# A hybrid encoder block on one core: modulation tiles added a step after their request, decay broadcasts pinned, solve copies reordered

## The chip, the cores and the metric

The kernel runs on one core of one Trainium2 chip. The metric is the device time of one execution in microseconds. A run of the kernel gives one time; several runs are compared by their median. One further execution was profiled, and its instructions, waits and transfers are what the views below show.

## The reference

One layer of a bidirectional encoder block for 256 tokens of width 2048, all in fp32:

```python
mod = silu(c) @ ada_w + ada_b          # 6 x 2048: shift, scale, gate for mixer and FFN
h = rms_norm(x, norm_mix_w) * (1 + scale_m) + shift_m
proj = h @ w_in                        # mLSTM q,k,v,o,i,f | delta rule q,k,v,z,beta,a | merge gates
y_a = mlstm_bidirectional(...) @ w_branch_a
y_b = gated_delta_bidirectional(...) @ w_branch_b
x = x + gate_m * ((g_a * y_a + g_b * y_b) @ w_out)
hf = rms_norm(x, norm_ffn_w) * (1 + scale_f) + shift_f
x = x + gate_f * ((silu(gt) * up) @ w_down)      # gt, up = split(hf @ w_gate_up)
return rms_norm(x, norm_final_w)
```

The delta rule has 16 heads of width 128. Per head and direction it needs a decay mask (products of the tokens' decays), the inverse of a unit triangular matrix per chunk, and products with the values.

## The kernel before, in words

**Weights.** Every weight arrives in chunks of 1 MB through three buffers with the tag `raw` (pool `st`), requested on the SP queue by `nc.sync.dma_start` (L156 in `fjob`, L183 in `tjob`). A chunk is turned into a high part by ScalarE (`wh`, L160 and L186) and a low part by VectorE (`wl`, L162 and L188), each in two halves, and TensorE takes three products per weight block (L165 to L167, L207 to L209). The SP queue issues its transfers in the order in which they are written, and a transfer into a buffer waits until the last reader of what lay there is done.

**Modulation.** The parts of `mod` that are needed later (2 to 5, sixteen tiles of 1 MB each) are made in the background. `ada_parts` requests a tile (L117) into one of the same three `raw` buffers and adds it: VectorE multiplies it with the row of silu(c) and sums along the row (L121). `pump`, called after each finished chunk, calls `sums` on every `every[0]`-th call, and this advances `ada_parts` by a tile. `room[0]` says which pool, how many buffers and how many tiles may be requested ahead: the `raw` buffers with depth 1 in the delta rule and the mLSTM part and again in the feed-forward part; a pool of its own (`sr`, three buffers, depth 3) between, while `y_a` and the output projection run. With depth 1, a tile's request and its addition are written one right after the other.

**The order of the work.** What is not pinned is placed by a planner, which puts the instructions of each engine in the order in which it expects them to be ready. `order(...)` (L71) pins an instruction behind everything already written for its engine. Small closures that must not be pinned too early are kept in the list `behind` (the SiLU after a convolution `end`, the copies of a triangle's corners `corners`, the norm of an output `scaled`), and `settle` (L130) writes out what the list holds; `fjob` and `tjob` call it between the two conversions of a half.

**The delta rule** (L868 to L917) treats four groups of four heads. `gdn_conv` (L287) prepares a projected head; for the first of its three projections it allots the decay buffer `al` (two of them) and calls `decay_load` (L282), which clears its edge and broadcasts the decays from DRAM, both on GpSimd (POOL), not pinned. `gdn_phase1` (L556) makes the masks by scans on VectorE (L562 to L565), the triangles (`mi`, `mb`), stores them (`inst`, L623) and reads them back in another layout (`uu`, L626), both from POOL. `gdn_invert` (L642) solves the four heads' small triangles on VectorE. `gdn_blocks` (L673) reads the result back, and copies it into `X` and `UL` (L692, L700), pinned on ScalarE. `gdn_phase2` (L703) works on a pair of heads in nine steps; the last one calls `settle()` (L795) and transposes the result. In the loop over `n` (L901) a step of the pair is written first, then a step of the block copies, then some pieces of the next heads' projections. `every[0]` is 0 in group 0 and in the inversions and 2 in groups 1 to 3.

**After it** come the mLSTM part with `y_b` (L1057 on), `y_a`, the output projection, and the feed-forward part from L1223.

Of the kernel before, what the change touches and what calls it, by code (L numbers as in the profile page):

```python
# [52 lines left out]
def hybrid_block(ctx: ExitStack, tc: tile.TileContext, xr, nfr, crow, pk_d, cst_d, ada2, ada4, win0, winb, wint, wba, wbb, wo, wgu, wd, out, dbg=None):  # L53
# [47 lines left out]
        order(S.activation(row_c[:, g * 512 : (g + 1) * 512], pc_, AF.Silu))  # L101


    room = [(st, "raw", 3, 1)]

    def ada_parts(*parts):

        todo = [(part, b) for part in parts for b in range(KB)]  # L110
        asked = []
        while todo or asked:
            pl, tag, bufs, depth = room[0]
            while todo and len(asked) < depth:
                part, b = todo.pop(0)
                raw = pl.tile([P, D], F32, tag=tag, bufs=bufs, name=f"ada{part}_{b}")
                nc.sync.dma_start(raw, ada4[part - 2, b])  # L117
                asked.append((part, b, raw))
            part, b, raw = asked.pop(0)
            c = part * KB + b  # L120
            V.scalar_tensor_tensor(raw, raw, 1.0, row_c[:, :D], ALU.mult, ALU.mult, accum_out=mod[:, c : c + 1])  # L121
            if b == KB - 1:
                c = slice(part * KB, part * KB + KB)
                V.tensor_tensor(mod[:, c], mod[:, c], pk[:, PK_ADAB + c.start : PK_ADAB + c.stop], ALU.add)
            yield True


    behind = []

    def settle(keep=0):  # L130

        while len(behind) > keep:
            behind.pop(0)()

    background = []
    count, every = [0], [0]
# [14 lines left out]
    def fjob(name, src, done):  # L151

        ps = acc_ps.tile([P, 512], F32, tag="acc", name=f"acc_{name}")
        o = ps[:, :T]
        raw = st.tile([P, KB, P], F32, tag="raw", bufs=3, name=f"raw_{name}")
        nc.sync.dma_start(raw, src)  # L156
        for k0 in range(0, KB, 8):
            wh = st.tile([P, 8, P], F32R, tag="wh", bufs=3, name=f"wh_{name}_{k0}")
            wl = st.tile([P, 8, P], F32R, tag="wl", bufs=3, name=f"wl_{name}_{k0}")
            S.activation(wh, raw[:, k0 : k0 + 8], AF.Copy)  # L160
            settle()
            V.tensor_tensor(wl, raw[:, k0 : k0 + 8], wh.bitcast(F32), ALU.subtract)  # L162
            for k in range(8):
                kk = k0 + k
                PE.matmul(o, wh[:, k], hh[:, kk], start=kk == 0, stop=False)  # L165
                PE.matmul(o, wh[:, k], hl[:, kk], start=False, stop=False)  # L166
                PE.matmul(o, wl[:, k], hh[:, kk], start=False, stop=kk == KB - 1)  # L167
            if k0:
                pump()
                done(o)  # L170
            yield True

    def tjob(name, chunks, xh, xl, done, early=0, by_token=None, steps=1):

        raws = {}

        def halves(u, k0):  # L180
            if u not in raws:
                raws[u] = st.tile([P, 4, 512], F32, tag="raw", bufs=3, name=f"raw_{name}_{u}")
                nc.sync.dma_start(raws[u], chunks[u])  # L183
            wh = st.tile([P, 2, 512], F32R, tag="wh", bufs=3, name=f"wh_{name}_{u}_{k0}")
            wl = st.tile([P, 2, 512], F32R, tag="wl", bufs=3, name=f"wl_{name}_{u}_{k0}")
            order(S.activation(wh, raws[u][:, k0 : k0 + 2], AF.Copy), early)  # L186
            settle()
            order(V.tensor_tensor(wl, raws[u][:, k0 : k0 + 2], wh.bitcast(F32), ALU.subtract), early)  # L188
            return wh, wl

        todo = [(u, k0) for u in range(len(chunks)) for k0 in (0, 2)]
        made = []
        for i, q in enumerate(todo[:early]):
            made.append(halves(*q))
            if steps > 1 or i == early - 1:
                yield True
        ps = [acc_ps.tile([P, 512], F32, tag="acc", name=f"acc_{name}_{t}") for t in range(2)]
        last = 4 * len(chunks) - 1
        if by_token:
            todo = todo[:-2]  # L200
        for n, (u, k0) in enumerate(todo):
            wh, wl = made.pop(0) if made else halves(u, k0)
            for k in range(2):
                kk = 4 * u + k0 + k
                for t in range(2):
                    c = slice(t * P, (t + 1) * P)
                    order(PE.matmul(ps[t], xh[:, kk, c], wh[:, k], start=kk == 0, stop=False), early and steps > 1)  # L207
                    PE.matmul(ps[t], xl[:, kk, c], wh[:, k], start=False, stop=False)  # L208
                    PE.matmul(ps[t], xh[:, kk, c], wl[:, k], start=False, stop=kk == last)  # L209
            if k0:  # L210
                pump()
                if u == len(chunks) - 1:
                    done(ps)
            yield True
            if early and steps > 1:
                if n + early < len(todo):
                    made.append(halves(*todo[n + early]))
                yield True
        if by_token:
            w = [halves(len(chunks) - 1, k0) for k0 in (0, 2)]  # L220
            by_token()
            for t in range(2):
                c = slice(t * P, (t + 1) * P)
                for k in range(4):
                    kk = last - 3 + k
                    wh, wl = (a[:, k % 2] for a in w[k // 2])
                    PE.matmul(ps[t], xh[:, kk, c], wh, start=False, stop=False)
                    PE.matmul(ps[t], xl[:, kk, c], wh, start=False, stop=False)
                    PE.matmul(ps[t], xh[:, kk, c], wl, start=False, stop=kk == last)
                done(t, ps[t])  # L230
                yield True
# [49 lines left out]

    def decay_load(h):  # L282
        al = parts[h][2]
        G.memset(al[:, :, 0:8], 0.0)
        G.dma_start(al[:, :, 8:], alpha_d[:, h].partition_broadcast(P))

    def gdn_conv(h, j, ps):  # L287

# [414 lines left out]
    def gdn_phase2(g, p):  # L703
# [88 lines left out]
            po, r4 = po2[:, 2 * e * P : 2 * (e + 1) * P], hd[e][4]  # L792
            ons.append(gdn_norm(g, h, hl_, po, r4))
        yield
        settle()  # L795
        for e, on in enumerate(ons):
            h, hl_ = 4 * g + 2 * p + e, 2 * p + e
            for t in range(2):
# [84 lines left out]
    def invert(g):  # L883
        gen = gdn_invert(g)
        next(gen)
        fill(4 if g else 6)
        for _ in gen:
            fill(1)

    invert(0)  # L890
    for g in range(4):
# [7 lines left out]
        for p in range(2):  # L899
            pieces = stream(4 * g + 2 * p + 4)  # L900
            for n in range(1, 10):  # L901
                next(pairs[p], None)
                if p == 0:
                    next(blocks, None)
                for _ in range(last[n] if g == 3 else second[n] if p else after[n]):
                    next(pieces)
            for _ in pairs[p]:
# [5 lines left out]
        if g < 3:  # L913
            fills.insert(0, z_job(g + 1))
            every[0] = 0
            invert(g + 1)
    settle()  # L917
    sx.close()
# [138 lines left out]
    cores = steps(mlstm(0), mlstm(1))  # L1057
    o4s = [o_load(g) for g in range(2)]
    every[0] = 0
    fill(2)  # L1060
    next(cores)
    fill(6)
# [23 lines left out]
    mgh, mgl = big(bigC, F32R, "mgh"), big(bigC, F32R, "mgl")  # L1086
    sm_.close()
    sr_ = ExitStack()
    room[0] = (pool(sr_, "sr"), "sr", 3, 3)
    for g in range(4):  # L1090
        every[0] = (2, 1, 1, 0)[g]
# [313 lines left out]
```

## Time and profile before

| | us |
|---|---|
| runs shown: median (lowest to highest, 3 runs) | 2083.49 (2080.6 to 2085.63) |
| profiled execution | 2082.03 |
| its span, first to last instruction | 2080.3 |
| mean granted TensorE clock in it | 0.992 |

PE is TensorE, PEld its weight loads, DVE VectorE, ACT ScalarE, SP the queue engine. In the timeline and the lists a row begins with the start in us from the beginning of the span and the duration in us; what stands in brackets at its end is the time that the engine stood idle ahead of it and what ended this wait. In the list of waits, the engine and line named first waited for what stands behind the arrow; the numbers are the total in us, how many times, and the longest. `L121` is line 121 of the kernel.

### The profile page before, as it was taken

The page shows a single profiled execution, that of the slowest core. Times are in us where ns is not written, and L with a number is a line of the kernel's source. Part 1 is how long each engine was busy: PE and PEld are TensorE (multiplying, and loading weights), DVE is VectorE, ACT ScalarE, POOL GpSimd, SP SyncE. Part 2 cuts the span into 40 slices and gives each one's busy share as a digit, 9 for nine tenths or more (in the row PEclk, how much of TensorE's full clock was granted, in tenths as well). Part 3 has the DMA queues.
Part 4 walks back from the last instruction along what each step waited for, and adds up shares of the span by engine and source line. Part 5 has one row for each costly group of instructions (what it writes and reads, how often), then busy time and mean ns, then how long its engine had stood idle before and what let it go on. Part 6 is the DMA issues. An engine that isn't in the chain of part 4 may idle for free.

```text
span 2080.3 us, 27020 instructions
## 1 busy us (share of the span) xinstructions
PE 2027.5 (97%) x10374; PEld 1698.8 (82%) x10374; DVE 1398.0 (67%) x2075; ACT 1033.1 (50%) x1551; POOL 116.8 (6%) x211
## 2 busy tenths in 40 slices
PE   8999999999999999999999999999999999999998
PEld 6777789978998988889777778788888888878886
DVE  6778877877887877765676976665655654455554
ACT  3147648756764766555344334454444444444443
POOL 0002210110111001101100000200000000000000
PEclk9999999999999999999999999999999999999999
DMA  9976664557766556667885976466666665555553
GB/s 401 420 316 201 193 230 160 162 191 247 245 205 206 210 197 223 233 230 271 310 300 184 397 300 228 145 224 234 239 235 230 239 239 195 188 201 185 200 187 137
DMA packets 78963, 485.65 MB, mean 233 GB/s; under 512 B 10585, under 2 KB 15969, under 8 KB 24433
## 3 DMA queue, kind: packets, MB, share of 16 engines
q1 hardware_dynamic: 63360, 450.95, 59.7%
q0 software_dynamic: 8160, 17.88, 3.8%
q10 hardware_dynamic: 7314, 15.10, 1.9%
q8 instruction: 81, 1.33, 0.3%
q14 instruction: 48, 0.39, 0.1%
HBM read 467.07 MB, written 16.82 MB: 233 GB/s over the span
## 4 chain that ended last, share of the span: by engine, by line
PE 73%; DVE 10%; DMA 9%; ACT 4%; issue 3%; POOL 0%; SPq 0%; ACTq 0%; DVEq 0%; POOLq 0%
PE acc_up L209 4%; PE acc_up L207 4%; PE acc_up L208 4%; PE acc_d L208 4%; PE acc_d L209 4%; PE acc_d L207 4%; PE acc_gt L207 4%; PE acc_gt L208 4%; PE acc_gt L209 4%; DMA ra<-ada 3%; PE acc_o L209 2%; PE acc_o L207 2%; PE acc_o L208 2%; PE acc_b L167 2%; PE acc_b L165 2%
## 5 line engine op out<-in xcount | busy, mean ns | idle before, releaser
L188 DVE TENSOR_TENSOR wl_d<-raw_d,wh_d 128x1024 fp32r<-128x1024 f32 x88 | 107.8, 1225 | 119.9 <-ACT wh_d L186 119.9
L188 DVE TENSOR_TENSOR wl_up<-raw_up,wh_up 128x1024 fp32r<-128x1024 f32 x88 | 107.6, 1225 | 110.5 <-ACT wh_up L186 110.5
L188 DVE TENSOR_TENSOR wl_gt<-raw_gt,wh_gt 128x1024 fp32r<-128x1024 f32 x88 | 107.8, 1225 | 91.0 <-ACT wh_gt L186 91.0
L165 PE MATMUL acc_b<-hh,wh_b 128*128 128x256 f32 x576 | 165.7, 288 | 1.5 <-ACT wh_b L160 1.5
L167 PE MATMUL acc_b<-hh,wl_b 128*128 128x256 f32 x576 | 161.9, 281 | 1.4 <-DVE wl_b L162 1.4
L121 DVE SCALAR_TENSOR_TENSOR ada<-ada,crow 128x2048 f32<-128x2048 f32 x64 | 146.2, 2286 | 24.3 <-DMA ada<-ada 24.3
L186 ACT ACTIVATE wh_d<-raw_d 128x1024 fp32r<-128x1024 f32 x88 | 93.3, 1061 | 139.0 <-PE acc_d L208 134.0
L166 PE MATMUL acc_b<-hl,wh_b 128*128 128x256 f32 x576 | 160.6, 279 | 0.0
L186 ACT ACTIVATE wh_gt<-raw_gt 128x1024 fp32r<-128x1024 f32 x88 | 93.3, 1060 | 128.7 <-PE acc_gt L208 77.2
L186 ACT ACTIVATE wh_up<-raw_up 128x1024 fp32r<-128x1024 f32 x88 | 93.2, 1060 | 116.4 <-PE acc_up L208 82.9
L207 PE MATMUL acc_gt<-wh_gt,hfh 128*128 128x512 f32 x352 | 139.6, 397 | 1.0 <-ACT hfh L1218 1.0
L208 PE MATMUL acc_gt<-wh_gt,hfl 128*128 128x512 f32 x352 | 138.9, 395 | 0.0
L209 PE MATMUL acc_gt<-wl_gt,hfh 128*128 128x512 f32 x352 | 137.7, 391 | 0.0
L208 PE MATMUL acc_up<-wh_up,hfl 128*128 128x512 f32 x352 | 136.9, 389 | 0.0
L207 PE MATMUL acc_up<-wh_up,hfh 128*128 128x512 f32 x352 | 136.9, 389 | 0.0
L209 PE MATMUL acc_up<-wl_up,hfh 128*128 128x512 f32 x352 | 136.8, 389 | 0.0
L207 PE MATMUL acc_d<-wh_d,ffh 128*128 128x512 f32 x344 | 134.3, 391 | 0.0
L208 PE MATMUL acc_d<-wh_d,ffl 128*128 128x512 f32 x344 | 134.3, 390 | 0.0
L209 PE MATMUL acc_d<-wl_d,ffh 128*128 128x512 f32 x344 | 133.9, 389 | 0.0
L530 PE MATMUL first<-x,raw 128*128 128x256 f32 x512 | 114.5, 382 | 6.8 <-ACT x L524 6.4
L530 PEld LDWEIGHTS first<-x,raw 128*128 128x128 f32 x512 | 96.0, 190 | 25.2 <-ACT x L524 12.8
L165 PEld LDWEIGHTS acc_b<-hh,wh_b 128*128 128x128 f32 x576 | 109.4, 190 | 2.3 <-ACT wh_b L160 1.6
(371 smaller groups left out, 5267.1 us busy)
## 6 DMA issues: line engine op xcount, KB each, us to landing
ada<-ada SPq DMA_DIRECT2D x64, 1024.0 KB, 5.2
raw_gt<-wgu SPq DMA_DIRECT2D x44, 1024.0 KB, 4.9
raw_up<-wgu SPq DMA_DIRECT2D x44, 1024.0 KB, 4.8
raw_d<-wd SPq DMA_DIRECT2D x44, 1024.0 KB, 4.8
raw_b<-winb SPq DMA_DIRECT2D x36, 1024.0 KB, 5.0
ra<-ada SPq DMA_DIRECT2D x32, 1025.0 KB, 15.4
raw<-win SPq DMA_DIRECT2D x16, 1024.0 KB, 14.5
raw_z<-wint SPq DMA_DIRECT2D x16, 1024.0 KB, 5.0
```

The lines of the kernel that those rows point to most:

```text
L121: V.scalar_tensor_tensor(raw, raw, 1.0, row_c[:, :D], ALU.mult, ALU.mult, accum_out=mod[:, c : c + 1])
L165: PE.matmul(o, wh[:, k], hh[:, kk], start=kk == 0, stop=False)
L166: PE.matmul(o, wh[:, k], hl[:, kk], start=False, stop=False)
L167: PE.matmul(o, wl[:, k], hh[:, kk], start=False, stop=kk == KB - 1)
L186: order(S.activation(wh, raws[u][:, k0 : k0 + 2], AF.Copy), early)
L188: order(V.tensor_tensor(wl, raws[u][:, k0 : k0 + 2], wh.bitcast(F32), ALU.subtract), early)
L207: order(PE.matmul(ps[t], xh[:, kk, c], wh[:, k], start=kk == 0, stop=False), early and steps > 1)
L208: PE.matmul(ps[t], xl[:, kk, c], wh[:, k], start=False, stop=False)
L209: PE.matmul(ps[t], xh[:, kk, c], wl[:, k], start=False, stop=kk == last)
L530: PE.matmul(first[o], raw[:, o], x[:, b], start=b == 0 and o % 2 == 0, stop=b == KB - 1 and o % 2 == 1)
```

## The change

The additions move into a function of their own, with a list `asked` that outlives a step. Where the depth is now 0 (the delta rule and the mLSTM part), a step of `ada_parts` first adds the tile that was requested a step earlier and then requests the next one. Where steps are far apart, `raw_tile`, through which the weights now get their buffers, writes the addition ahead of the third buffer after the request; it is also written ahead of each further inversion, at the start of the mLSTM part and ahead of `y_a`. `decay_load` is pinned on POOL. The last step of a pair settles only the closures named `scaled`. In the loop over `n`, the step of the block copies comes ahead of the pair's.

```diff
-    room = [(st, "raw", 3, 1)]
+    room = [(st, "raw", 3, 0)]
+    asked, since = [], [0]
+
+    def add():
+        part, b, raw = asked.pop(0)
+        c = part * KB + b
+        V.scalar_tensor_tensor(raw, raw, 1.0, row_c[:, :D], ALU.mult, ALU.mult, accum_out=mod[:, c : c + 1])
+        if b == KB - 1:
+            c = slice(part * KB, part * KB + KB)
+            V.tensor_tensor(mod[:, c], mod[:, c], pk[:, PK_ADAB + c.start : PK_ADAB + c.stop], ALU.add)
 
     def ada_parts(*parts):
         todo = [(part, b) for part in parts for b in range(KB)]
-        asked = []
         while todo or asked:
             pl, tag, bufs, depth = room[0]
-            while todo and len(asked) < depth:
+            if not depth and asked:
+                add()
+            while todo and len(asked) < max(depth, 1):
                 part, b = todo.pop(0)
                 raw = pl.tile([P, D], F32, tag=tag, bufs=bufs, name=f"ada{part}_{b}")
                 nc.sync.dma_start(raw, ada4[part - 2, b])
                 asked.append((part, b, raw))
-            part, b, raw = asked.pop(0)
-            ...
+                since[0] = 0
+            if depth:
+                add()
             yield True
 
+    def raw_tile(shape, name):
+        since[0] += 1
+        if since[0] > 2 and asked and room[0][0] is st:
+            add()
+        return st.tile(shape, F32, tag="raw", bufs=3, name=name)
+
-    def settle(keep=0):
-        while len(behind) > keep:
-            behind.pop(0)()
+    def settle(keep=0, only=None):
+        now = [f for f in behind if only is None or f.__name__ == only]
+        for f in now[: len(now) - keep]:
+            behind.remove(f)
+            f()
 ...
-        G.memset(al[:, :, 0:8], 0.0)
-        G.dma_start(al[:, :, 8:], alpha_d[:, h].partition_broadcast(P))
+        order(G.memset(al[:, :, 0:8], 0.0))
+        order(G.dma_start(al[:, :, 8:], alpha_d[:, h].partition_broadcast(P)))
 ...
-        settle()
+        settle(only="scaled")
         for e, on in enumerate(ons):
 ...
             for n in range(1, 10):
-                next(pairs[p], None)
                 if p == 0:
                     next(blocks, None)
+                next(pairs[p], None)
 ...
         if g < 3:
             fills.insert(0, z_job(g + 1))
             every[0] = 0
+            if asked:
+                add()
             invert(g + 1)
```

Two more `if asked: add()` stand ahead of the mLSTM part's first `fill(2)` and ahead of the change of `room[0]` to the pool `sr`; `fjob` and `tjob` call `raw_tile` in place of `st.tile`.

More of the change, by code (lines that the diff above doesn't have):

```diff
@@ L118, in ada_parts @@
                 asked.append((part, b, raw))
-            part, b, raw = asked.pop(0)
[L120 to L124, printed above, removed]
-            yield True
-    behind = []
-    def settle(keep=0):
-        while len(behind) > keep:
-            behind.pop(0)()
+                since[0] = 0
+            if depth:
+                add()
+            yield True
+    def raw_tile(shape, name):
[3 more added lines that the diff above has]
+        return st.tile(shape, F32, tag="raw", bufs=3, name=name)
+    behind = []
+    def settle(keep=0, only=None):
[3 more added lines that the diff above has]
+            f()
     background = []
@@ L154, in fjob @@
         o = ps[:, :T]
-        raw = st.tile([P, KB, P], F32, tag="raw", bufs=3, name=f"raw_{name}")
+        raw = raw_tile([P, KB, P], f"raw_{name}")
         nc.sync.dma_start(raw, src)
@@ L181, in halves @@
             if u not in raws:
-                raws[u] = st.tile([P, 4, 512], F32, tag="raw", bufs=3, name=f"raw_{name}_{u}")
+                raws[u] = raw_tile([P, 4, 512], f"raw_{name}_{u}")
                 nc.sync.dma_start(raws[u], chunks[u])
@@ L1059, in hybrid_block @@
     every[0] = 0
+    if asked:
+        add()
     fill(2)
@@ L1088, in hybrid_block @@
     sr_ = ExitStack()
+    if asked:
+        add()
     room[0] = (pool(sr_, "sr"), "sr", 3, 3)
```

## The prediction

> **What bounds the kernel now.** I read the page first, then one table of windows by stage, then the chain of waits in the stages that the edit touches.
>
> ```profile
> PE 2027.5 (97%) x10374; PEld 1698.8 (82%) x10374; DVE 1398.0 (67%) x2075; ACT 1033.1 (50%) x1551; POOL 116.8 (6%) x211
> 480.00:600.00 120.00, 118.03 (x887) 109.50 (x886) 100.68 (x184) 84.66 (x168) 11.28 (x22) 1.00 0.69 234
> 600.00:680.00 80.00, 78.51 (x439) 67.08 (x439) 61.28 (x128) 42.11 (x65) 11.26 (x22) 1.00 0.63 202
> 680.00:800.00 120.00, 117.10 (x876) 109.82 (x875) 95.58 (x182) 84.15 (x171) 8.86 (x17) 0.97 0.60 211
> ...
> 870.00:970.00 100.00, 97.75 (x569) 85.06 (x570) 60.07 (x85) 56.23 (x109) 0.00 (x0) 0.98 0.66 234
> 970.00:1138.00 168.00, 162.66 (x714) 126.84 (x713) 110.30 (x150) 72.27 (x100) 14.70 (x24) 0.97 0.73 268
> ```
>
> The first line is the page's total; TensorE (PE) is busy 97% of the span. The window rows give a stretch and its length, then the busy time of PE, its weight loads, VectorE (DVE), ScalarE (ACT) and POOL, then the granted PE clock, the DMA share and GB/s. The modulation tiles with the new order are requested between 480 and 1138 us (none in 800 to 863). In these rows PE is idle 1.97 + 1.49 + 2.90 + 2.25 + 5.34 = 14.0 us, and the clock below 1.00 costs another 0.03 x 120 + 0.02 x 100 + 0.03 x 168 = 10.6 us. So some 25 us, 1.2% of the time, is all that the edit could ever win. What it could lose has no such ceiling. Next: where in these stages the loss sits.
>
> ```profile
> 740.00:760.00 20.00, 17.76 (x141) 17.36 (x140) 15.86 (x31) 12.91 (x27) 2.70 (x5) 0.91 0.48 175
> 760.00:780.00 20.00, 20.00 (x161) 19.87 (x161) 13.80 (x25) 13.05 (x23) 0.00 (x0) 0.92 0.61 211
> 860.00:880.00 20.00, 18.27 (x100) 15.57 (x99) 11.95 (x15) 9.11 (x16) 2.00 (x4) 0.91 0.65 230
> 980.00:1000.00 20.00, 16.74 (x71) 13.52 (x70) 11.26 (x12) 7.49 (x8) 4.85 (x9) 0.96 1.02 390
> 1000.00:1020.00 20.00, 20.00 (x90) 16.70 (x89) 13.53 (x21) 9.06 (x12) 2.53 (x4) 0.86 0.82 308
> ```
>
> The worst place in the delta rule is 740 to 780: 2.24 us idle, and a clock of 0.91 and 0.92 that costs 0.09 x 20 + 0.08 x 20 = 3.4 us. The chain of waits tells what came ahead of it:
>
> ```profile
> 729.93 2.22 DVE ada L121 x2
> 732.17 8.68 DMA raw_b<-winb
> ...
> 746.69 2.21 DVE ada L121 x2
> 748.90 1.14 DVE wl_b L162
> ```
>
> Read it downward: an addition of a modulation tile (ada, L121) ends, and only then can a weight transfer start in the buffer it leaves; the transfer takes 8.68 us, and later a second addition stands 2.21 us ahead of the conversion (wl_b, L162) that PE wants. Both additions are what the edit moves.
>
> **The change, part by part.**
>
> *The additions.* Their number stays; the last 16 of them lie in the feed-forward part, where the depth is still 1 and the order is as it was. No work is removed or added.
>
> ```profile
>   DMA ada<-ada: 24.3, 14
> SPq L156 <- DVE ada L121: 50.2, 11, 10.4
> SPq L183 <- DVE ada L121: 83.7, 30, 10.8
> 1016.67 2.29 DVE L121 SCALAR_TENSOR_TENSOR ada<-ada,crow 128x2048 f32<-128x2048 f32 x1 [4.70 <-DMA ada<-ada]
> ```
>
> One addition is 2.29 us of DVE. It made DVE stand still 24.3 us in 14 waits for its own transfer (first line, idle before the addition), the longest 4.70 us at 1016.67. The two SPq lines count the other side: 41 times a weight transfer on the SP queue was released by an addition. That queue issues in order, so everything behind such a transfer waits too. After the edit an addition is written two weight chunks later, behind both chunks' conversions, so it should no longer stand ahead of a conversion, but it also gives its buffer back later.
>
> By stage. *680 to 800:* I take the 2.24 us gap and the 3.4 us of clock as won, **-5.6 us**; bounds from -6.5 (all idle and clock of the stage, 2.90 + 3.6) to a loss that the first rival prices. *480 to 600:* an addition stands in the chain here too (515.14):
>
> ```profile
> 515.14 1.18 DVE ada L121
> 894.15 5.78 DMA ada<-ada
> 976.71 18.97 DMA bc<-mal_d
> ```
>
> Of 1.97 us idle I take a third, **-0.7** (bounds 0 and -1.97). *870 to 970:* most of the 2.25 us idle is the 1.73 in 860 to 880, where the solve's result is read back; what the ada transfer at 894.15 ends is the smaller rest, **-0.4** (0 to -0.5). *970 to 1138:* the 3.26 us idle in 980 to 1000 belongs to the broadcast of the mLSTM decay (18.97 us) and stays. The rest is 5.34 - 3.26 = 2.1 us idle and a clock loss of 0.14 x 20 = 2.8 us in 1000 to 1020, in which the 4.70 us wait lies. DVE is otherwise under-used here (110.30 of 168), so an addition may well keep its place; I take a third, **-1.6** (0 to -4.9).
>
> *Price of the later release.* Between 680 and 800 a modulation tile's buffer is wanted by the next weight transfer almost at once:
>
> ```profile
> ACT wh_b L160 <- DMA raw_b<-winb: 8.1, 5, 4.3
> 679.70 0.33 SPq L117 DMA_DIRECT2D ada<-ada  x1
> ...
> 748.93 1.47 SPq L156 DMA_DIRECT2D raw_b<-winb  x2
> ...
> 783.25 0.33 SPq L117 DMA_DIRECT2D ada<-ada  x1
> ```
>
> ACT stood still 8.1 us in 5 waits for such transfers, so there is little slack. An addition behind one more pair of conversions (wl_b, 2 x 1.14 us) releases 2.3 us later. I charge this once as exposed, **+2.3 us**; the bounds are 0 (the release at 748.93 is followed within 1.2 us by a second one from a converted chunk, which could serve instead) and the first rival's sum.
>
> *Decay broadcasts held behind the triangles.* The memset and the DMA of a head's decay (al) are pinned on POOL behind all that is written ahead of them.
>
> ```profile
> 215.56 0.52 POOL L626 DMA_DIRECT2D uu<-inst_d  x1 [1.74 <-DMA inst_d<-mi]
> ...
> 616.21 2.18 POOL L623 DMA_DIRECT2D inst_d<-mi  x4 [13.61 <-DVE mi L617]
> 620.40 0.11 POOL L284 MEMSET al<- 128x16 f32 x1 [2.01 <-DVE dec L565]
> ...
> 621.58 0.52 POOL L626 DMA_DIRECT2D uu<-inst_d  x1
> DMA to landing us min/median/max: 5.1/7.0/9.6
> ```
>
> At 620.40 the memset of a later head waits for a decay buffer, and the triangle's reload (uu, L626), which the inversion on DVE needs, is issued behind it at 621.58. Where no broadcast stood between, the reload followed the stores by 1.74 us (215.56), which would be 616.21 + 2.18 + 1.74 = 620.13 here: 1.45 us earlier. PE's 1.49 us idle in 600 to 680 follows this inversion. I take **-1.0** (0 to -1.5 in this group). What the move delays: each broadcast now queues behind a reload that itself waits for DMA, and needs 7.0 us (median) to land. It is needed only after the head's three projections, so I cost that at nothing; without that cover one head could wait up to 9.6 us of DVE, at the start of three groups.
>
> *Settling only the norm's closures, and the solve copies ahead of the pairs.* No instruction is added; the six copies of the corners and the copies into X and UL change their place on ACT.
>
> ```profile
> 744.82 0.26 ACT L633 ACTIVATE cc<-mi 32x64 f32<-32x64 f32 x1 [2.07 <-DVE mi L607]
> ```
>
> At 744.82 the corners' copies (0.26 us for one) held ACT 2.07 us for DVE, ahead of a weight conversion. That belongs to the same gap as above and is already in the 5.6; elsewhere I count 0, with bounds of one such wait, 2.07 us, won or lost.
>
> **Sum:** -5.6 - 0.7 - 0.4 - 1.6 + 2.3 - 1.0 = **-7.0 us**. The profiled execution took 2082.03 us (span 2080.3), so 2075.0 there; the median of the runs shown is 2083.49, 1.5 above it, so on that footing the forecast is **2076.5 us**.
>
> A rule to weigh against this. The half-rate stretches above followed idle times that sum to 2.24 us (740 to 760) and 1.73 us (860 to 880). The Trainium skill, page "TensorE: Matmul & The Clock Gate", section "What's actually happening", says that the clock falls to half after at least one idle window of about 3.4 us that runs freely; these rows show falls with less idle time, so the trace does not agree and decides. By that page alone the gap would not be the cause of the fall, the 3.4 us would stay, and the sum would be -3.6 us instead of -7.0.
>
> **The rivals.**
>
> *Slower: the late additions starve the weight buffers.* In 680 to 800 eight modulation tiles pass through the three buffers (the requests from 679.70 to 783.25). If each addition is put behind one more pair of conversions, each release is 2.3 us later, 18.4 us together. The next weight transfer can take either the tile's buffer or a converted chunk's, so I count half, 9.2 us; PE then idles longer and one more fall of the clock costs another 3.4 us. The won 5.6 does not come. With the other stages' gains (-0.7 - 0.4 - 1.6 - 1.0 = -3.7) this is 9.2 + 3.4 - 3.7 = +8.9: **2092.4 us**. It decides once an addition starts more than the 1.2 us between the two releases at 748.93 later than today. For it: the 41 releases by additions, the 8.68 us transfer in the chain. Against: a starved DVE goes idle, and the addition is ready and can run then.
>
> *No change: the additions stay where they were.*
>
> ```profile
> 513.91 1.23 DVE L162 TENSOR_TENSOR wl_b<-raw_b,wh_b 128x1024 fp32r<-128x1024 f32 x1
> 515.06 2.28 DVE L121 SCALAR_TENSOR_TENSOR ada<-ada,crow 128x2048 f32<-128x2048 f32 x1
> 517.67 1.22 DVE L162 TENSOR_TENSOR wl_b<-raw_b,wh_b 128x1024 fp32r<-128x1024 f32 x1
> ```
>
> The instructions that the kernel does not pin are already issued out of the order in which they are written: here an addition sits between conversions, although the old text puts it behind a whole job. If the planner places an addition when it believes the tile has landed, writing it later changes nothing where DVE is free, and the 24.3 us of waits stay. Then only the POOL edit remains, -1.0: **2082.5 us**. For it: the 4.70 us wait came with no other work ready on DVE, and there the written order would not matter. Against: in 680 to 800 DVE had other work queued (95.58 of 120 us), so there the written order does matter.
>
> *The gap closes, the clock stays low.* If the 3.4 us of clock between 740 and 780 do not come back, because other idle time in the same stretch trips it, the sum is -3.6: **2079.9 us**.
>
> **How the numbers follow.** This kernel's measurement can tell about 0.2%, 4.2 us, from no change. Forecast and its neighbours below 2079.3: 0.44. Additions unmoved, 0.14, and clock stays low, 0.07: 0.21 within 0.2%. Starved buffers: 0.35. The likeliest case alone spans 2070 to 2079. The whole range reaches from 2069.5 (twice the forecast gain, over half of the 25 us ceiling) to 2096 (the starved case with a little more than its price); I leave out about 0.05 below and 0.12 above.
>
> **What would show it.** Right: between 680 and 800 no additions directly ahead of weight conversions in the chain of waits, PE idle under 1 us, clock 1.00; DVE's wait for ada transfers well below 24.3 us; in the third inversion the reload follows its stores without a memset between. Wrong: ACT's waits for raw_b transfers above 8.1 us, more SP releases by additions or longer ones, or a further stretch with a clock near 0.91. It would be wrong altogether if the planner reorders much more than the edited lines, so that gaps appear in stages that I left out (300 to 480, 1138 to 1240).

## The result, and the profile after

The changed kernel takes 2093.38 us (median of 5 runs, 2092.27 to 2096.76), the kernel before 2083.49 us beside it (5 runs, 2080.6 to 2087.38). The ratio is 1.0051, with an interval of 1.0036 to 1.0067: **slower by half a per cent**, where the forecast said 2076.5 us. The profiled execution took 2092.5 us (span 2090.4, mean granted clock 0.991).

The first view of the kernel after is the table of windows, for the stages that the prediction used (columns as there):

```profile
480.00:600.00 120.00, 114.11 (x823) 104.49 (x822) 93.51 (x165) 81.20 (x154) 11.16 (x24) 1.00 0.68 229
600.00:680.00 80.00, 80.00 (x489) 70.60 (x488) 63.40 (x142) 43.98 (x75) 13.45 (x26) 1.00 0.61 205
680.00:800.00 120.00, 113.60 (x839) 105.54 (x838) 93.58 (x178) 76.96 (x158) 7.47 (x15) 0.96 0.62 208
870.00:970.00 100.00, 97.55 (x557) 83.97 (x556) 57.90 (x77) 55.45 (x108) 2.01 (x4) 1.00 0.69 247
970.00:1138.00 168.00, 162.80 (x767) 130.44 (x766) 109.99 (x148) 71.90 (x95) 14.72 (x24) 0.98 0.76 279
```

PE's idle time rose from 1.97 to 5.89 us in 480 to 600 and from 2.90 to 6.40 us in 680 to 800, and it fell from 1.49 us to nothing in 600 to 680. So two stages lose, and one gains; 870 to 970 also gains 2.0 us of clock (0.98 to 1.00). The stretches are fixed in time and the changed kernel runs 4 to 13 us late in them, so a row holds nearly, but not exactly, the same work as before. The list of waits of the kernel after names what is new:

```profile
DVE dec L580 <- DMA al<-alpha_d: 24.0, 7, 6.0
DVE ada L111 <- DMA ada<-ada: 21.8, 14, 4.1
ACT wh_b L178 <- DMA raw_b<-winb: 12.6, 7, 5.1
SPq L201 <- DVE ada L111: 78.9, 28, 10.7
SPq L174 <- DVE ada L111: 52.5, 13, 9.2
```

The lines of the kernel have moved (L562 is now L580, L121 L111, L160 L178, L183 L201, L156 L174). The first row is the find: the scans that make a head's decay masks stood 24.0 us for the broadcast `al`, seven times. In the list of waits of the kernel before that row is this one, a single wait of the very first head:

```profile
DVE dec L562 <- DMA al<-alpha_d: 2.7, 1, 2.7
```

The additions' waits for their tiles, on the other hand, hardly moved (24.3 to 21.8, 14 times in both), nor did the releases by additions. To see what a scan's wait costs, take the second pair of heads. In the kernel before, POOL issues head 2's broadcast as soon as head 0's scans have freed the buffer, at 177.76 us:

```profile
177.72 0.11 POOL L284 MEMSET al<- 128x16 f32 x1 [4.48 <-DVE dec L565]
177.76 0.77 POOL L285 DMA_DIRECT2D al<-alpha_d  x1
```

In the kernel after, the timeline of POOL has nothing there. The broadcasts of heads 2 and 3 both stand behind the last reload of the pair before:

```profile
214.58 0.52 POOL L644 DMA_DIRECT2D uu<-inst_d  x1 [1.75 <-DMA inst_d<-mi]
215.08 0.13 POOL L302 MEMSET al<- 128x16 f32 x1
215.13 0.74 POOL L303 DMA_DIRECT2D al<-alpha_d  x1
215.87 0.13 POOL L302 MEMSET al<- 128x16 f32 x1
215.92 0.72 POOL L303 DMA_DIRECT2D al<-alpha_d  x1
```

The reload itself waits for its stores, as the prediction said. And then the chain of waits after (start, duration, what):

```profile
215.13 8.37 DMA al<-alpha_d
...
223.52 0.70 DVE dec L580
...
225.43 1.13 DVE wl_v L206
```

On DVE the four scans stand ahead of a weight conversion (`wl_v`), which starts when the last of them ends, and PE waits for the conversion. The same place, and a second one 160 us later, in windows of 20 us, first after, then before:

```profile
220.00:240.00 20.00, 17.20 (x66) 12.13 (x66) 14.60 (x36) 9.15 (x17) 2.74 (x5) 0.91 0.58 181
380.00:400.00 20.00, 18.07 (x146) 17.87 (x145) 13.86 (x21) 10.75 (x20) 0.69 (x2) 0.91 0.52 166
```

```profile
220.00:240.00 20.00, 20.00 (x88) 15.59 (x88) 15.09 (x39) 10.80 (x21) 3.46 (x7) 1.00 0.79 218
380.00:400.00 20.00, 19.98 (x177) 19.82 (x176) 14.49 (x25) 14.83 (x27) 0.00 (x0) 1.00 0.60 176
```

A wait of 4.83 us by DVE left PE idle 2.80 us at 220 to 240, and the clock of 0.91 took another 1.8; at 380 to 400 it is 1.91 us more idle and 1.8 of clock. Both lie in stages that the prediction left out. The longest gap of PE lies in one that it did count, behind the scans of head 14, which waited 6.04 us; its window had PE busy 20.00 us and a clock of 0.92 before:

```profile
760.00:780.00 20.00, 15.56 (x117) 15.36 (x117) 10.65 (x17) 10.30 (x18) 0.00 (x0) 0.83 0.51 158
769.29 0.58 PE L185 MATMUL acc_b<-hh,wl_b 128*128 128x256 f32 x1 [4.44 <-DVE wl_b L180]
```

Of the six pinned scans that waited, five have such a gap of PE right behind them: 2.81, 1.93, 2.32, 0.61 and 4.44 us for heads 2, 6, 10, 12 and 14 (head 4 has none). That is 12.1 us together, where the whole span is 10.1 us longer.

How the delay grows and shrinks can be read by taking the start of the first conversion of the same weight chunk in both traces, after minus before (my own subtraction):

| first chunk of | before, at us | delay, us |
|---|---|---|
| `mb0`, mLSTM weights | 261.0 | +2.2 |
| head 4 | 303.4 | +4.3 |
| head 6 | 364.9 | +1.2 |
| head 7, second chunk | 388.4 | +5.1 |
| head 9 | 508.2 | +5.5 |
| head 11 | 566.7 | +9.2 |
| `z2`, at the third inversion | 607.5 | +10.1 |
| head 12, behind it | 675.2 | +7.2 |
| `z3`, at the fourth inversion | 801.5 | +11.6 |
| feed-forward part | 1318.6 | +10.2 |

So the loss is made ahead of 810 us, in steps; part comes back by head 6, and 2.9 us come back over the third inversion. Behind the fourth inversion nothing of note is added.

### The profile page after: what moved, and what is told of

Read it like the earlier page. It is cut to its first block, busy times and chain, and to the rows that moved or that the text cites. A ratio compares the mean times of both kernels' runs of the same rounds, so it can differ in the third digit from the quotient of the medians.

```text
span 2090.4 us, 26994 instructions
## 1 busy us (share of the span) xinstructions
PE 2029.7 (97%) x10374; PEld 1702.4 (81%) x10374; DVE 1397.5 (67%) x2075; ACT 1033.5 (49%) x1551; POOL 116.1 (6%) x211
## 4 chain that ended last, share of the span: by engine, by line
PE 75%; DMA 10%; DVE 9%; issue 2%; ACT 2%; POOL 1%; ACTq 0%; SPq 0%; DVEq 0%; POOLq 0%
PE acc_up L227 4%; PE acc_up L225 4%; PE acc_up L226 4%; PE acc_d L226 4%; PE acc_d L225 4%; PE acc_d L227 4%; PE acc_gt L225 4%; PE acc_gt L226 4%; PE acc_gt L227 4%; DMA ra<-ada 3%; PE acc_o L227 2%; PE acc_o L225 2%; PE acc_o L226 2%; PE acc_b L183 2%; PE acc_b L185 2%
## 5 line engine op out<-in xcount | busy, mean ns | idle before, releaser
L183 PE MATMUL acc_b<-hh,wh_b 128*128 128x256 f32 x576 | 166.6, 289 | 0.0
L111 DVE SCALAR_TENSOR_TENSOR ada<-ada,crow 128x2048 f32<-128x2048 f32 x64 | 146.3, 2287 | 22.0 <-DMA ada<-ada 21.8
L227 PE MATMUL acc_d<-wl_d,ffh 128*128 128x512 f32 x344 | 133.9, 389 | 0.0
L185 PEld LDWEIGHTS acc_b<-hh,wl_b 128*128 128x128 f32 x576 | 109.8, 191 | 6.3 <-DVE wl_b L180 6.2
```

## The experiments

Three theories stood at the start. **T1**: the pinned broadcasts land too late for their scans. **T2** (the prediction's first rival): late additions starve the weight buffers. **T3**: the order of `settle` and of the copies matters. Each run below lasted five rounds beside the kernel before. Ratios are to the kernel before on the same chip; its median was 2082.52 us for the first four runs, 2084.11 for the next four, then 2080.75, 2082.67 and 2084.09, so ratios are to be compared and not the times.

### The three parts, one at a time

*All of the change without the pins*, that is `order(...)` taken off the memset and the broadcast.

> The changed kernel with the decay broadcasts no longer pinned on POOL; everything else of the change stays. Theory 1 (the pinned broadcasts cost the time: the scans wait 24.0 us in 7 waits for al, where they waited 2.7 us in one): the whole loss of some 10 us goes, 2080 to 2085 us, the scans' waits for al fall to about 3 us. Theory 2 (the late additions starve the weight buffers): the loss stays, 2090 us or more. Theory 3 (settling and the copies' order): the loss stays too.

Measured: 2088.36 us, ratio 1.0019 [1.0002, 1.0036]. That is above the 2080 to 2085 us of T1: more than half of the loss goes, and what stays is as much as the additions' new code costs alone (1.0018, below). *The pins alone*, on the kernel before:

```diff
-        G.memset(al[:, :, 0:8], 0.0)
-        G.dma_start(al[:, :, 8:], alpha_d[:, h].partition_broadcast(P))
+        order(G.memset(al[:, :, 0:8], 0.0))
+        order(G.dma_start(al[:, :, 8:], alpha_d[:, h].partition_broadcast(P)))
```

> The kernel before with the two pins on the decay broadcast alone. Theory 1: 2091 to 2096 us, with idle time of VectorE ahead of the scans of some 20 us and idle TensorE near the scans of heads 2, 6, 10 and 14. Theory 2 and theory 3: within 3 us of 2083.5.

Measured: 2096.07 us, ratio **1.0068 [1.0045, 1.0090]**. *The additions' new code alone*:

> The kernel before with the additions' new place alone. Theory 1: the additions hardly move in the issue order, so within 4 us of 2083.5, with ada waits near 24 us. Theory 2: 2090 us or more, with longer waits for raw_b transfers than the 8.1 us of before. My forecast's own step would have it at 2077 to 2079.

Measured: 2086.95 us, ratio 1.0018 [1.0004, 1.0032]. *`settle(only="scaled")` and the block copies ahead of the pairs, alone*:

> The kernel before with the last step of a pair settling only the norm's closures and the block copies written ahead of the pair's step; additions and broadcasts as before. Theory 1 and theory 2: within 3 us of 2083.5. Theory 3: 2090 us or more.

Measured: 2083.01 us, ratio 1.0000 [0.9987, 1.0013].

The two lines of pins cost alone about what the whole change does (1.0068, with an interval that overlaps that of 1.0051). Their waits, in the run with the pins alone:

```profile
DVE dec L562 <- DMA al<-alpha_d: 25.8, 7, 6.6
DVE ada L121 <- DMA ada<-ada: 21.3, 15, 3.8
ACT wh_b L160 <- DMA raw_b<-winb: 15.4, 7, 7.6
```

The scans wait again seven times, with additions and copies as before. T1 is shown, together with the gaps of PE above; T3 counts nothing. The parts do not add up: the pins cost 0.68% on the kernel before, and some 0.3% on top of the other two parts (1.0051 against 1.0019). The single ratios' intervals are too wide to say more of this, and I leave it open. The additions' new code costs 0.18% by itself. The sign of T2 came with it (ACT's waits for `raw_b` 12.1 us, before 8.1), its time of 2090 us or more did not. Compared instruction by instruction, one addition of 64 stands at another place among the weight conversions in that run, by half a chunk, and five of 64 in the changed kernel. The planner puts an addition where it put it before. The delay of that run is 0.5 us at head 10 and 4.1 us at head 11 and at the end; which of the reshuffled instructions there costs it was not tried.

### Pins, but early, and pins for half of the heads

*The broadcast of head h+2 written directly behind head h's scans, and pinned there.* It then waits only for a buffer that has just come free.

```diff
+        if h + 2 < NH_B:
+            decay_tile(h + 2)
+            decay_load(h + 2)        # memset and broadcast, both pinned
```

> The kernel before with the broadcast pinned, but written right behind the scans of head h for head h + 2 (they free the buffer), so ahead of the triangle's stores and some tens of us ahead of its own scans. Theory 1 (a broadcast that is pinned behind the reload lands too late for the scans): the scans' waits for al fall from 25.8 us to about 3, and the time goes back to 2080 to 2086 us. Rival (the pin itself or the two broadcasts' bandwidth costs the time, not the lateness): 2090 us or more.

Measured: 2086.69 us, ratio 1.0011 [0.9997, 1.0025]. The scans' waits for `al` are down to the first head's 2.2 us, and so is most of the loss: 1.0068 became 1.0011. What is left is a delay that begins with a gap of PE at 216.66 us. I put that gap down to the broadcast, which stood among the triangles' stores, and tested that with *the same, but heads 2 to 5 not pinned*:

> The kernel before with one edit: the memset and the broadcast of head h+2 are written directly behind head h's scans, and they are pinned to that place from head 6 on; heads 2 to 5 stay free, additions and settle as before. T1 (a pinned broadcast costs because it lands behind its scan, and in the start because it takes the queue from the first weights): no scan waits over 2 us for al any more, no gap of PE near 216 us, the inversions at 600 to 680 and behind keep what the earlier broadcast frees (PE without idle time there): 2079 to 2084 us. Rival (the pinning costs by the stretch of time in which the transfer lands, among the weights, however early): 2086 us or more, with waits of the weight conversions on raw_b over 12 us as in the other pinned kernels. The forecast's own step for the broadcasts (-1.0 us, nothing lost) would give 2082.5.

Measured: 2085.74 us, ratio 1.0017 [1.0007, 1.0026]. The gap is still there, at 218 us, so this reading falls. The rival's sign came too: ACT's waits for `raw_b` are 13.0 us. But the delay against the kernel before is 6.0 us at `mb0` already, and shrinks to 0.8 us by the end of the profiled execution, so what is left is made at the start and not by those waits. DVE's timeline of this run, then that of the kernel before, show what the gap is:

```profile
209.51 1.22 DVE L188 TENSOR_TENSOR wl_v<-raw_v,wh_v 128x1024 fp32r<-128x1024 f32 x1
...
214.53 1.63 DVE L313 SCALAR_TENSOR_TENSOR cv<-pad,pk,cv 128x256 f32<-128x256 f32 x4
216.08 0.68 DVE L569 TENSOR_TENSOR_SCAN dec<-al,cst 128x256 f32<-128x256 f32 x1
216.68 1.65 DVE L313 SCALAR_TENSOR_TENSOR cv<-pad,pk,cv 128x256 f32<-128x256 f32 x4
...
220.26 3.47 DVE L188 TENSOR_TENSOR wl_v<-raw_v,wh_v 128x1024 fp32r<-128x1024 f32 x3
```

```profile
211.28 2.42 DVE L307 SCALAR_TENSOR_TENSOR cv<-pad,pk,cv 128x256 f32<-128x256 f32 x6
213.62 1.22 DVE L188 TENSOR_TENSOR wl_v<-raw_v,wh_v 128x1024 fp32r<-128x1024 f32 x1
214.75 0.87 DVE L307 SCALAR_TENSOR_TENSOR cv<-pad,pk,cv 128x256 f32<-128x256 f32 x2
...
218.55 2.33 DVE L188 TENSOR_TENSOR wl_v<-raw_v,wh_v 128x1024 fp32r<-128x1024 f32 x2
```

No transfer is waited for. In the kernel before, a weight conversion stands among the convolution's taps (`cv`) at 213.62 us, and the next at 218.55. With the broadcast written earlier, the planner puts that conversion ahead of the triangles (`mi`, `mb`), at 209.51 us, and then none until three in a row at 220.26. The high part of the first of these was done at 211.78 us, and PE stood idle 3.08 us until its low part was there. This is a cost of the order on DVE, not of landing; why the planner chose it was not tried. *With the settle and the copies beside it*:

> The run before this one (broadcasts early, pinned from head 6 on) with the change's third part beside it: settle for the scaled copies alone, and the solve's block copies ahead. That part alone gave 1.0000. If the two add up, the time is within 1.5 us of the run before this one, so 2078 to 2084 us under T1; a difference over 3 us between the two would show that copies and broadcasts meet on the same engines.

Measured: 2082.4 us, ratio 1.0010 [0.9998, 1.0022]: 3.3 us below the run without them, which would speak for a part of their own, but the two intervals overlap, so this run decides nothing. *Pins, at their late place, only for the first pair of each group, and only for the second*:

> The kernel before with the broadcast pinned for heads 0, 1, 4, 5, 8, 9, 12 and 13 alone, the first pair of each group. In the kernel with all pins, VectorE waited 3.07 and 2.21 us for heads 4 and 12. Theory 1: about a third of the pins' cost, 2 to 5 us more than before. Rival (bunched broadcasts take bandwidth from weight transfers, the same in each pair): half, about 7 us.

> The kernel before with the broadcast pinned for the second pair of each group alone (heads 2, 3, 6, 7, 10, 11, 14, 15), where VectorE waited 4.83, 2.82, 2.88 and 6.04 us. Theory 1: two thirds or more of the pins' cost, 7 to 12 us more than before. Rival: about 7 us, as much as the other half.

Measured: 2089.24 us, 1.0030 [1.0017, 1.0043], with 10.0 us of scan waits in three; and 2091.22 us, 1.0044 [1.0028, 1.0060], with 18.5 us in five. Taken by their scans' waits (2.2, 10.0, 18.5 and 25.8 us) the ratios are 1.0011, 1.0030, 1.0044 and 1.0068. The cost follows the waits, at four points. The two halves alone do not decide against their rival (bunched broadcasts take bandwidth, about 7 us in each half), since their intervals overlap; what speaks for the waits is that PE's gaps stand right behind the late scans.

### What the additions cost, and what the forecast's step was worth

*The additions held for real where the new code writes them*:

```diff
-        V.scalar_tensor_tensor(raw, raw, 1.0, row_c[:, :D], ...)
+        order(V.scalar_tensor_tensor(raw, raw, 1.0, row_c[:, :D], ...), not room[0][3])
```

> The additions' part of the change alone, and with it each addition of the delta rule and the mLSTM part is held to the place at which the new code writes it (in the change itself the planner is free and 59 of 64 stay where they were). It tells what the forecast's step was worth had it happened. The forecast (PE's gaps behind late ada tiles go: 5.6 us at 680 to 800, 0.7, 0.4 and 1.6 us elsewhere, 2.3 us paid back): 2077 to 2079 us, ada waits of VectorE below 5 us in sum. Rival A (a tile that is held one or two chunks longer holds one of three weight buffers, so the next weight request is late): 2090 us or more, the weight conversions' waits on raw_b over 15 us, and waits of the weight queue for additions of more than the 50 and 84 us of before.

Measured: **2128.09 us, ratio 1.0213 [1.0192, 1.0233]**. The sign that the forecast named came true, and the time went the other way. Its waits, then two of the kernel before, then its windows at the stretch where 30 us are lost (the delay grows from 7.5 us at head 12 to 38 us at `z3`):

```profile
DVE ada L111 <- DMA ada<-ada: 5.7, 4, 3.2
ACT pad L320 <- PE acc_b L185: 41.5, 18, 7.4
ACT wh_yb L204 <- DMA raw_yb<-wbb: 36.1, 7, 7.4
```

```profile
ACT pad L302 <- PE acc_b L167: 2.6, 4, 0.9
ACT wh_yb L186 <- DMA raw_yb<-wbb: 5.5, 2, 3.5
```

```profile
700.00:720.00 20.00, 17.51 (x142) 16.43 (x142) 13.06 (x22) 11.48 (x22) 0.00 (x0) 1.00 0.38 136
720.00:740.00 20.00, 16.17 (x112) 14.70 (x112) 12.90 (x30) 10.73 (x30) 3.50 (x7) 0.91 0.34 95
740.00:760.00 20.00, 18.07 (x99) 13.90 (x97) 16.82 (x41) 10.54 (x23) 0.00 (x0) 1.00 0.76 275
...
800.00:820.00 20.00, 16.45 (x132) 15.03 (x130) 16.55 (x35) 12.68 (x31) 2.68 (x5) 1.00 0.31 98
```

VectorE's waits for tiles fell from 24.3 to 5.7 us, because the tiles now lie there long before they are added. But while they lie there they hold one of three buffers: the last column falls to 136, 95 and 98 GB/s in three of these windows, where the kernel before had 204, 262 and 246. SP's queue shows the stop:

```profile
714.32 0.33 SPq L129 DMA_DIRECT2D ada<-ada  x1
716.53 12.19 SPq L174 DMA_DIRECT2D raw_b<-winb  x2
740.32 0.33 SPq L129 DMA_DIRECT2D ada<-ada  x1
742.92 0.33 SPq L201 DMA_DIRECT2D raw_mb<-wint  x1
```

Between 728.7 and 740.32 us nothing is requested. That looks like T2, the forecast's first rival, in the place that it named. But the trace shows a second cause beside it, and in this stretch a larger one. The chunk requested at 716.53 had landed at 722.3 us, and its conversion began only at 734.90 us. Until 734.60 us ScalarE stood idle for 7.42 us ahead of the copy of a finished projection (`pad`), which waits for PE, and the conversion stood behind that copy. From 680 to 840 us such waits sum to 30.2 us in ten (before 1.7), ScalarE's waits for weight transfers to 12.8 us (before 7.7). The signs expected for T2 stayed away: `raw_b` waits are 9.1 us and not over 15, and the queue's waits for additions fell to 28.5 and 63.6 us. Only in y_b does ScalarE wait much longer for weights (36.1 us), and there the delay does not grow (32 us at its start, 33 us in `y_a`). So the additions held to these places cost some 44 us (2.13% of 2083), where the rival's sum was +8.9; how much of it is the held buffer and how much the order that the planner then gave ScalarE was not separated. *Short additions* (64 of 2048 columns), transfers as before:

> The kernel before with each addition of the delta rule and the mLSTM part run over 64 of its 2048 columns (the rest of those sums is left out), all transfers as before. Without tiles and additions the kernel took 12.9 us less; this splits that. If VectorE's time in the additions is what costs (some 30 additions, each over 2 us on the engine that the scans and the solve need): 2072 to 2076 us. If the arrival of the tile and the weight buffer that it holds is what costs: 2080 to 2084 us, since the waits for tiles and the requests stay.

Measured: 2071.39 us, ratio 0.9954 [0.9941, 0.9968]. *No tiles and no additions* in the same parts:

> The kernel before without the 30 modulation tiles of the delta rule and the mLSTM part: they are neither transferred nor added (their columns of mod stay zero), so this leaves out part of the computation. It bounds what any order of the additions could win there. My forecast's step (tiles and additions cause the idle time and the low clock of 680 to 800 and a part elsewhere): 8 us or more less than before. Rival (these stages' idle time belongs to the delta rule's own chain): within 4 us of before.

Measured: 2071.49 us, ratio 0.9938 [0.9922, 0.9953]. The two intervals overlap. So most of what the additions cost is their 2.29 us each on VectorE (and the buffer for that time): with short ones PE's idle time in 680 to 800 falls from 2.90 to 0.70 us, though VectorE still waits 16.1 us for tiles in all. The transfers, and the buffers until the addition starts, cost little on top where nothing holds the additions back. From these two runs I estimate that about half a per cent is all that any placement of the additions could win here.

### Can the place of the additions win it?

Both runs leave work out. These leave nothing out and take the eight additions of 680 to 800 us elsewhere (`every[0]`): into y_b; into the fourth group, and two into y_a; into y_a; those of 480 to 600 too, into y_b and y_a; and into the stretch between the fourth group and y_b.

```diff
-        every[0] = (0, 2, 2, 2)[g]
+        every[0] = (0, 2, 0, 2)[g]
...
-    every[0] = 2
+    every[0] = 1
     fills[:] = [y_bs()]
```

> The kernel before with none of the eight additions that it has between 680 and 800 us; eight more stand in the y_b products from 970 us on (one at every chunk there instead of at every second). Nothing is left out. The forecast's step put 5.6 us of PE's idle time and low clock between 680 and 800 on tiles that come late to an addition. If an addition costs there and not where VectorE has room, the stretch of 680 to 800 gains 4 to 7 us as in the runs without tiles or with short additions, and the whole takes 2076 to 2080 us. Rival (an addition costs its time wherever it stands before the MLP): 2081 to 2086 us, with the loss back between 970 and 1138.

> As the run with eight additions moved into y_b, but they go to the fourth group (870 to 970 us, an addition at every chunk instead of at every second: six more) and to y_a (two more). If an addition is free where no head's columns stream, 2076 to 2080 us. Rival (the fourth group's own scans and solve lose what 680 to 800 gains): 2081 us or more with gaps of PE between 870 and 970.

> As the run with eight additions moved into y_b, but six go to y_a (one at every chunk) and two to the drain in the output product. If additions cost nothing behind 1138 us: 2076 to 2080 us. Rival (y_a and the output product are where VectorE and the weight buffers are tightest): 2083 us or more, with the loss at 1138 to 1300.

> The eight additions of 480 to 600 us and the eight of 680 to 800 us both moved: y_b takes one at every chunk, y_a one at every chunk, and the last two are drained in the output product. Nothing is left out. If the ceiling shown by the run with no tiles (12.9 us) lies in these two stretches, 2072 to 2078 us; if the products behind 970 us pay for what they take, 2080 us or more, above all at 1138 to 1300, where VectorE is busy 127 of 162 us already.

> The kernel before with none of the eight additions of 680 to 800 us; those that are missing go between the fourth group and the y_b products (some 943 to 1000 us, one at every chunk there, where the kernel before has none), and what is then still missing into the drain in the output product. Nothing is left out. If that stretch has room for them (VectorE is busy 55 of 100 us between 900 and 1000), the 4 to 5 us gained at 680 to 800 stay: 2076 to 2079 us. Rival (the eight additions cost about the same in every stretch before the MLP, as the runs with y_b, the fourth group and y_a suggest): 2080 to 2086 us.

| eight additions go to | us | ratio |
|---|---|---|
| y_b | 2080.58 | 0.9990 [0.9977, 1.0003] |
| the fourth group and y_a | 2086.06 | 1.0012 [0.9998, 1.0026] |
| y_a and the drain | 2094.04 | 1.0054 [1.0035, 1.0074] |
| y_b and y_a (sixteen) | 2093.21 | 1.0056 [1.0037, 1.0074] |
| between the fourth group and y_b | 2089.0 | 1.0030 [1.0016, 1.0044] |

The windows of the y_b run tell why:

```profile
680.00:800.00 120.00, 119.09 (x896) 110.66 (x895) 85.90 (x181) 88.17 (x179) 8.93 (x17) 1.00 0.48 155
...
970.00:1138.00 168.00, 160.92 (x680) 123.91 (x680) 125.11 (x163) 68.91 (x98) 13.81 (x23) 0.96 0.85 317
```

Between 680 and 800 PE's idle time falls from 2.90 to 0.91 us and the clock is full, 5.6 us in all; y_b then loses 1.7 us of PE and 0.01 of the clock, and the whole ends within 0.2% of the kernel before. In the y_a run, 1138 to 1300 is where it is lost:

```profile
1138.00:1300.00 162.00, 148.10 (x640) 117.92 (x639) 139.88 (x155) 61.34 (x72) 0.00 (x0) 0.98 0.89 347
```

PE is busy 148.10 us there, against 155.16 in the kernel before. An average share of VectorE says little: the stretch between the fourth group and y_b looked free and was not. Last, *that place with the early broadcasts and the copies*:

> The same place for the additions, with the broadcasts written early and pinned from head 6 on, and the third part of the change (settle for the scaled copies alone, block copies ahead). The broadcasts and copies alone gave 1.001; the place of the additions adds to that, so this lies within 2 us of the run before it. Rival (an earlier broadcast and a queue without tiles meet: the weights are requested further ahead in 680 to 800, so the broadcast's landing is later): 3 us or more above it.

Measured: 2094.9 us, ratio 1.0056 [1.0037, 1.0075], about 5 us above the run without them and more than was expected, though the two intervals overlap. No scan waits but the first head's 3.5 us, so late landing is not the reason; the cause stays open. **No version that does all the work beats the kernel before** by more than can be measured; the y_b run (0.9990) is the nearest.

## Why the prediction was wrong, point by point

**Decay broadcasts: the step that failed.** The prediction gave the earlier reload -1.0, and for the delayed broadcast said "I cost that at nothing; without that cover one head could wait up to 9.6 us of DVE, at the start of three groups". The reload's part was right in kind: PE's idle time in 600 to 680 went from 1.49 us to none, and the delay shrank by 2.9 us over the third inversion. The cover was not there. In the kernel before a broadcast is issued as soon as the buffer is free, so it has landed 16 to 124 us ahead of its scan for every head but the first. Pinned behind the reload, it lands 0.02 us ahead of its scan for six heads, the first of a pair each (2, 4, 6, 10, 12 and 14), and not only at the start of three groups. With the very first head's, that makes seven waits, 24.0 us of DVE; behind five of them PE stood idle 12.1 us, and the pins alone cost +0.68%. The median to landing, on which the step leaned (7.0 us), also rose to 8.5, now that the two broadcasts of a pair are issued back to back:

```profile
DMA to landing us min/median/max: 5.2/8.5/11.8
```

**Additions, -5.6, -0.7, -0.4, -1.6 and +2.3.** None of these came as forecast, because the additions hardly moved: five of 64 changed place, and DVE's waits for tiles are 21.8 us in 14. The second rival ("the planner places an addition when it believes the tile has landed") had this mechanism right; its time, 2082.5, left out the broadcasts. The size of the gap was right as well: with no additions in 680 to 800 that stretch does gain 5.6 us. But the way to it was wrong. In the one run that held them later, the time grew by 2.1%. The tile that comes late was read as the cause of the gap; the run with short additions, in which VectorE still waits for tiles, shows that its 2.29 us for each is.

**The slower rival** said 2092.4 us, 1 us from the result, for another reason than the true one: the nearness is luck. The releases by additions hardly changed in the changed kernel (28 and 13, before 30 and 11; 131.4 us of waits, before 133.9). When the additions are held, a loss of its direction comes and is five times its sum, but in the stretch that it named it is made more by ScalarE's order than by late weights.

**Settle and copies, 0.** Right: 1.0000 [0.9987, 1.0013].

**The clock.** The changed kernel falls to half clock behind idle times of 2.80 us (220 to 240) and 1.93 us (380 to 400): matmuls that start every 0.11 us ahead of the second gap start every 0.21 us behind it, until 391.9 us. This agrees with what the prediction took from the trace, against the Trainium skill, page "TensorE: Matmul & The Clock Gate", section "What's actually happening", with its 3.4 us of idle time; no run here tells why so short a gap does it. Behind a gap of 2.32 us at 580.61 us the clock stays at 1.00 in the window from 580 to 600.

**What would have told it.** Of the signs named, ACT's waits for `raw_b` above 8.1 us (12.6) and gaps in the stages left out (220 to 240, 380 to 400, both with a clock of 0.91) both came true. The first is a poor one, though: it came in the kernel with the additions alone as well (12.1 us), and in the early pins (13.5 and 13.0 us), which cost next to nothing.

## What to carry to other kernels

Ahead of pinning a transfer behind something, look up its slack: its landing against the start of its first reader, for every instance in the trace; a median to landing says nothing of that, and the price is what stands behind the reader on its engine. A wait that goes away (tiles 24.3 to 5.7 us) can cost much more than it was, when the pin that removes it holds a shared buffer and changes the order on other engines. And what an order written by hand does is to be seen in the issue order first: a planner may not move the instruction at all, or move others.

## What the hardware showed unexpectedly

A transfer of the heads' weights (`raw_b`, 1 MB) took 12.2 us at the longest in the changed kernel, and 8.7 in the kernel before, with a median of 4.9 and 5.0. The longest one is in the chain of waits after, issued at 490.86 us, behind two broadcasts at 487.96 and 488.74 us of 256 KB each, and beside another weight transfer (the second longest, 11.8 us at 295.75, also follows two, at 293.83 and 294.62 us):

```profile
490.86 12.19 DMA raw_b<-winb
```

That the broadcasts delay it was not tested by itself. The runs with pins show longer `raw_b` waits (12.6 and 15.4 us, with 8.1 before), but so does the run with additions alone (12.1), which has none, so broadcasts cannot be the only reason.
